# A two-layer decoder trunk on TensorE: other run lengths of high and low products, and another offset of three operand tiles

## The chip, the cores and the metric

The kernel runs on one core of one Trainium2 chip. A core has TensorE (PE in the profile; PEld is its weight load), VectorE (DVE), ScalarE (ACT), GpSimd (POOL) and SyncE (SP), which issues the transfers of the weights. The metric is the time of one execution on the device in microseconds; the time before is 2203.13 us, the median of three runs from 2200.47 to 2203.22.

## The reference

A trunk of two layers over 256 positions of width 2048, in float32. The first layer mixes by attention in a sliding window (32 query heads of 64, 8 key heads), the second by a gated linear recurrence; each ends with a gated MLP of width 6144 with a causal convolution over three positions.

```python
for layer in range(DEPTH):
    h = rmsnorm(x, mix_norm[layer])
    if layer % 2 == 0:
        x = x + sliding_window_attention(h, w_qkv, q_gain, k_gain, sinks, w_o)
    else:
        x = x + rglru_block(h, w_in, conv_w, conv_b, w_a, b_a, w_i, b_i, lam, w_out)
    h = rmsnorm(x, ffn_norm[layer])
    u = causal_dwconv(h @ w_up, conv_w, conv_b)
    g, v = split(u, 2)
    x = x + (gelu(g) * v) @ w_down
```

Nearly all the arithmetic is in the matrix products with w_qkv, w_o, w_in, w_out, w_up and w_down.

## The kernel before

Activations are held with the channels on the 128 partitions and the 256 positions (`T`) along the free axis, so a product takes a 128 x 128 block of weights as the stationary operand and streams the activations past it. To keep float32 precision at PE's faster rate, each operand is split in two float32r parts, a high one (the value cast down) and a low one (what the cast lost). An activation tile has both side by side: `h[:, k]` is 2 x 256 columns, high and low. A product of weights and activations is then two matmuls for each block k:

- a **high product** (`mm_hi`, L186 to L190): the high weights against both parts of the activations, 512 columns, into the 512 columns of one bank of the accumulator;
- a **low product** (`mm_lo`, L192 to L196): the low weights against the high part of the activations, 256 columns, added into the second half of the same bank.

Weights come in **chunks** of 128 x 2048 numbers (1 MB, 8 KB on a partition), 16 blocks each, in one fixed list `order` for the whole kernel. Each chunk goes through three steps, each with a ring of three buffers: SP issues its transfer into a `raw` tile (`dma_next`), ScalarE casts it to `hi` (`split_hi`, L115), VectorE subtracts to get `lo` (`split_lo`, L123). `advance()` does one step of each for the chunks ahead. A `hi` tile's buffer is written again for the chunk three later, after PE has read it for the last time. The order of the instructions on each engine is the order in which the program is written (`manual_schedule`); nothing is reordered by a scheduler.

The sections that the change touches, in the order of the program:

- `po`, the output projection of the attention, with `ao` as activations: chunks 2 to 15 of 16 in a plain loop, one chunk for each output block. The first two are interleaved with the end of the attention.
- `pu`, the up projection of the MLP, with `h`: two halves of 24 pairs of chunks (a gate and a value block), each pair into the two banks of one accumulator tile. In the first half the first pair is taken by `late_pair`, which leaves the last two blocks for after the norm. Each chunk is 16 high products, then 16 low ones; then comes a piece of the pair before (`step(pend)`, the epilogue `up_epi`: scale, convolution, gelu, and the split of the result into `g`), `advance()`, and another piece.
- `pd`, the down projection behind each half, with `g` as activations: eight accumulator tiles of two banks, three chunks each. A chunk has eight blocks k for each of the two banks (`i`): eight high products and eight low ones for the first bank, then eight and eight for the second. Its epilogue adds to the residual stream `x`.
- `px` and `py`, the input projections of the recurrence, with `h`, among its gates; the change leaves them as they are.
- `pr`, the output projection of the recurrence, with `z`, like `po`; then the second layer's `pu` and `pd`.

Tiles stand in SBUF in the order in which the pools are opened. In the built program `h` starts at byte 17536 of a partition (a multiple of 128), the three `hi` tiles at 86592, 94784 and 102976 and the `lo` tiles behind them (each 64 past a multiple of 128), and the pools of a section start at 135744, so that `g` is at 135744, `ao` at 160320 and `z` at 186944 (each 64 past one). The attention's smaller tiles lie behind `ao` and `z`'s place: `kq` takes 4 bytes of a 32-byte step, and the tiles `ident`, `identr`, `maskr`, `pt`, `pr`, `qsq` and `qh` behind it start on multiples of 128. All sizes along the way are multiples of 512 for the blocks of weights and of 2048 for those of activations.

Of the kernel before, what the change touches and what calls it, by code (L numbers as in the profile page):

```python
# [19 lines left out]
F32 = mybir.dt.float32  # L20
F32R = mybir.dt.float32r
AF = mybir.ActivationFunctionType
ALU = mybir.AluOpType
AX = mybir.AxisListType

P = 128
# [14 lines left out]
def trunk(ctx, tc, xT, wq, wk, wv, wo, win, wg, wout, wup, wdn, mixg, ffng, kqg, sinks,  # L41
# [9 lines left out]
    rawp = ctx.enter_context(tc.tile_pool(name="rawp", bufs=3))  # L51
    hip = ctx.enter_context(tc.tile_pool(name="hip", bufs=3))
    lop = ctx.enter_context(tc.tile_pool(name="lop", bufs=3))
    ctx.enter_context(tc.manual_schedule())

    x = per.tile([P, KD, T], F32, name="x")
# [13 lines left out]
    sp = per.tile([P, KD], F32, name="sp")  # L70
    sp4 = per.tile([P, KD], F32, name="sp4")
    sp8 = per.tile([P, KD], F32, name="sp8")


    order = []
# [117 lines left out]
    def mm_lo(ps, lo, rhs, ks, off=0, n=P, stop=True):  # L193
        for k, xk in ks:
            pe.matmul(ps[:, T:], lhsT=lo[:, off + k * n:off + k * n + P], rhs=rhs[:, xk, 0, :],  # L195
                      start=False, stop=stop and k == ks[-1][0])  # L196

    def x_epi(ps, d, n, gains, tp, out_=None, tag="xt"):

        t = tp.tile([P, n, T], F32, tag=tag, name=f"xt{st['use']}")  # L200
        xs = x[:, d:d + n, :]
        for i in ([slice(0, n)] if out_ is None else [slice(i, i + 1) for i in range(n)]):
            dve.tensor_tensor(out=t[:, i], in0=ps[:, i, 0:T], in1=xs[:, i], op=ALU.add)  # L203
            dve.tensor_tensor(out=xs[:, i], in0=ps[:, i, T:], in1=t[:, i], op=ALU.add)  # L204
            if out_ is not None:
                nc.sync.dma_start(out=out_[:, d:d + n, :][:, i], in_=xs[:, i])
        if out_ is not None:
            return
        yield
        if gains is None:  # L210
            return
        for i in range(d, d + n):
            split_x(h, x[:, i, :], gains, i)
        yield
        if n == 2:
            stat(xs, d == 0)
        elif d % 2:
            stat(x[:, d - 1:d + 1, :], d == 1)
# [35 lines left out]
    def rng(a, b):  # L254
        return [(k, k) for k in range(a, b)]
# [27 lines left out]
    with ExitStack() as ph:  # L283
# [7 lines left out]
        kz = ap_.tile([P, 4, 2, 2, T], F32R, name="kz")  # L291
        vh = ap_.tile([P, 2, 2, 512], F32R, name="vh")
        ao = ap_.tile([P, KD, 2, T], F32R, name="ao")
        kq = ap_.tile([P, 1], F32, name="kq")
        kg = ap_.tile([P, 2], F32, name="kg")
        snk = ap_.tile([P, 32], F32, name="snk")
        nsnk = ap_.tile([P, 32], F32, name="nsnk")
        cb = ap_.tile([P, T], F32, name="cb")
# [83 lines left out]
        def k_fin(p):  # L382
            s, sq = ksq.pop(p)
            pk = psT.tile([P, 512], F32, tag="pT", name=f"pk{p}")
            pe.matmul(pk[:, 0:T], lhsT=bones, rhs=sq, start=True, stop=True)
            yield
            v = a2.tile([P, T], F32, tag="ka", name=f"kv{p}")
            r = a2.tile([P, T], F32, tag="kr", bufs=1, name=f"kr{p}")
            t = a2.tile([P, T], F32, tag="kt", bufs=1, name=f"kt{p}")
            dve.scalar_tensor_tensor(out=v, in0=pk[:, 0:T], scalar=1.0 / HD, in1=cb, op0=ALU.mult, op1=ALU.add)  # L390
            rsqrt1(r, v)
            yield
            rsqrt2(r, v, t)
            dve.scalar_tensor_tensor(out=s, in0=s, scalar=kq[:, 0:1], in1=r, op0=ALU.mult, op1=ALU.mult)
            yield
            for i in range(2):
                sl = slice(64 * i, 64 * i + 64)
                act.copy(out=kz[sl, p, 0, i, :], in_=s[sl])
                dve.tensor_tensor(out=kz[sl, p, 1, i, :], in0=s[sl], in1=f(kz[sl, p, 0, i, :]), op=ALU.subtract)
# [249 lines left out]
                yield from x_epi(ps.unsqueeze(1), d, 1, gf[:, 0], a2, tag="ks")  # L649

        pend = wo_epi([(d, head[d][0]) for d in range(2)])
        for d in range(2, 16):
            hi, lo = use()
            ps = pj.tile([P, 512], F32, tag="pj", name=f"po{d}")
            mm_hi(ps, hi, ao, rng(0, KD))
            mm_lo(ps, lo, ao, rng(0, KD))
            step(pend)
            advance()
            finish(pend)
            if d == 8:  # L660
                softplus()
            pend = wo_epi([(d, ps)])
# [11 lines left out]
    def ffn(layer, nxt):  # L674
        with ExitStack() as ph:
            gp = ph.enter_context(tc.tile_pool(name=f"ffn{layer}", bufs=1, reuse_waits="tile"))
            t2 = ph.enter_context(tc.tile_pool(name=f"ffnt{layer}", bufs=2, reuse_waits="tile"))
            g = gp.tile([P, KH, 2, T], F32R, name=f"g{layer}")
            rbb = rb.unsqueeze(1).to_broadcast([P, 2, T])

            def up_epi(t, m, ps):
                a = t2.tile([P, 2, T], F32, tag="a", name=f"ua{layer}_{t}")
                s = t2.tile([P, 2, T], F32, tag="s", name=f"us{layer}_{t}")
                y = t2.tile([P, 2, T], F32, tag="y", name=f"uy{layer}_{t}")
                act.copy(out=a, in_=ps[:, :, 0:T])  # L685
                dve.tensor_tensor(out=s, in0=ps[:, :, T:], in1=a, op=ALU.add)  # L686
                dve.tensor_tensor(out=s, in0=s, in1=rbb, op=ALU.mult)  # L687
                yield
                for i in range(2):
                    n = t + i * (DFF // P)  # L690
                    act.activation(out=y[:, i, :], in_=s[:, i, :], func=AF.Identity, scale=fw[:, layer, n, 2:3],  # L691
                                   bias=fb[:, layer, n:n + 1])
                    for tap in (1, 2):
                        dve.scalar_tensor_tensor(out=y[:, i, tap:], in0=s[:, i, 0:T - tap],  # L694
                                                 scalar=fw[:, layer, n, 2 - tap:3 - tap], in1=y[:, i, tap:],
                                                 op0=ALU.mult, op1=ALU.add)
                yield
                yield
                act.activation(out=y[:, 0, :], in_=y[:, 0, :], func=AF.Gelu_apprx_tanh)
                dve.tensor_tensor(out=s[:, 0, :], in0=y[:, 0, :], in1=y[:, 1, :], op=ALU.mult)  # L700
                act.copy(out=g[:, m, 0, :], in_=s[:, 0, :])  # L701
                dve.tensor_tensor(out=g[:, m, 1, :], in0=s[:, 0, :], in1=f(g[:, m, 0, :]), op=ALU.subtract)  # L702

            pend = None
            for half in range(2):
                for m in range(KH):
                    t = half * KH + m
                    ps = mm.tile([P, 2, 512], F32, tag="mm", name=f"pu{layer}_{t}")
                    if t == 0:
                        late_pair(ps, h, lambda: norm(f"f{layer}"))  # L710
                    else:
                        for i in range(2):
                            hi, lo = use()
                            mm_hi(ps[:, i], hi, h, rng(0, KD))
                            mm_lo(ps[:, i], lo, h, rng(0, KD))
                            step(pend)
                            advance()
                            step(pend)
                    finish(pend)
                    pend = up_epi(t, m, ps)  # L720
                for dp in range(8):
                    ps = mm.tile([P, 2, 512], F32, tag="mm", name=f"pd{layer}_{half}_{dp}")
                    for c in range(3):
                        hi, lo = use()
                        ks = [(kk, 8 * c + kk) for kk in range(8)]
                        for i in range(2):
                            mm_hi(ps[:, i], hi, g, ks, off=i * P, n=2 * P, start=c == 0)
                            mm_lo(ps[:, i], lo, g, ks, off=i * P, n=2 * P, stop=c == 2)
                        step(pend)
                        advance()  # L730
                        step(pend)
                        if c == 1:
                            finish(pend)
                    pend = x_epi(ps, 2 * dp, 2, nxt if half else None, t2, None if half == 0 or nxt is not None else out)
            finish(pend)
# [3 lines left out]
    with ExitStack() as ph:  # L739
# [157 lines left out]
        for q, (what, n) in enumerate(rec_pairs):  # L897
# [10 lines left out]
                    run(after.get((q, i), ()))  # L908
            (xps if what == "x" else yps)[n] = ps

        pend = None
        for n in range(8):
            ps = mm.tile([P, 2, 512], F32, tag="mm", name=f"pr{n}")
            if n == 0:
                yproj(7)
                gated(7)
                zsplit(7)
                late_pair(ps, z)
            else:
                for i in range(2):  # L920
                    hi, lo = use()
                    mm_hi(ps[:, i], hi, z, rng(0, KD))
                    mm_lo(ps[:, i], lo, z, rng(0, KD))
                    step(pend)
                    advance()
                    step(pend)
            finish(pend)
            pend = x_epi(ps, 2 * n, 2, gf[:, 1], r2, tag="y")
# [66 lines left out]
```

## Time and profile before

| what | us |
|---|---|
| median of three runs | 2203.13 |
| the profiled execution | 2203.18 |
| its span, from the first instruction to the last | 2201.4 |
| PE busy | 2185.1 |
| VectorE busy | 1559.6 |
| ScalarE busy | 1182.0 |
| GpSimd busy | 134.0 |

The granted TensorE clock is 0.998 of full speed over the span. The weights, 401.06 MB read, come at 183 GB/s. A transfer of a chunk lands about 4.8 us after its issue. In a row of the profile `pu<-h,hi` is a matmul that writes the accumulator tile `pu` from the moving tile `h` and the stationary tile `hi`; `128x512 f32` is the size of the moving operand. The busy time of PE is not the distance from one matmul to the next: matmuls are pipelined, and a high product that is shown with 392 ns starts some 229 ns after the one before it. Distances are read from the starts in the timeline.

### The profile page before, as it was taken

How to read it: one execution, taken by the hardware profiler on the slowest of the kernel's cores; microseconds unless marked ns; L12 is line 12 of the kernel's file. 1: busy time of each engine (PE TensorE's matmuls, PEld its weight loads, DVE VectorE, ACT ScalarE, POOL GpSimd, SP SyncE). 2: the span in 40 equal slices, each digit the busy share in tenths (PEclk: the TensorE clock that was granted, in tenths of full speed). 3: DMA queues.
4: the chain of work that ended last, by engine and by line, in shares of the span. 5: the costliest groups of instructions: out<-in, count | busy, mean ns of one | idle time of the engine just before them, and what ended most of it. 6: DMA issues, size and time to landing. Idle time of an engine off the chain costs nothing.

```text
span 2201.4 us, 30745 instructions
## 1 busy us (share of the span) xinstructions
PE 2185.1 (99%) x12676; PEld 1922.7 (87%) x12676; DVE 1559.6 (71%) x1882; ACT 1182.0 (54%) x1432; POOL 134.0 (6%) x125
## 2 busy tenths in 40 slices
PE   9999999999999999999999999999999999999999
PEld 7788888888888888888888888888888888888888
DVE  6777768777644777776679877777776457777654
ACT  6677445555433555553369874455554335555432
POOL 1112220000000000002200003200000000000000
PEclk9999999999999999999999999999999999999999
DMA  7223555555555555555555546555555555555543
GB/s 272 101 96 115 192 177 206 191 191 191 191 192 188 180 192 189 191 200 183 189 211 184 186 154 213 181 194 191 191 192 191 191 177 191 191 190 191 193 187 134
DMA packets 60763, 405.14 MB, mean 184 GB/s; under 512 B 7504, under 2 KB 9936, under 8 KB 12880
## 3 DMA queue, kind: packets, MB, share of 16 engines
q1 hardware_dynamic: 60336, 403.04, 51.3%
q8 instruction: 99, 1.62, 0.3%
q14 instruction: 40, 0.33, 0.0%
q10 hardware_dynamic: 288, 0.15, 0.0%
HBM read 401.06 MB, written 2.10 MB: 183 GB/s over the span
## 4 chain that ended last, share of the span: by engine, by line
PE 98%; DVE 1%; ACT 0%; DMA 0%; issue 0%; SPq 0%; DVEq 0%
PE pu L189 32%; PE pu L195 16%; PE pd L189 16%; PE pd L195 8%; PE px L189 3%; PE py L189 3%; PE pr L189 3%; PE po L189 3%; PE pq L189 2%; PE pr L195 1%; PE po L195 1%; PE py L195 1%; PE px L195 1%; PE pq L195 1%; PE O L574 1%; PE pk L189 1%
## 5 line engine op out<-in xcount | busy, mean ns | idle before, releaser
L123 DVE TENSOR_TENSOR lo<-raw,hi 128x2048 fp32r<-128x2048 f32 (+1 forms) x390 | 856.5, 2196 | 213.7 <-ACT hi L115 206.8
L115 ACT CAST hi<-raw 128x2048 fp32r<-128x2048 f32 x373 | 712.7, 1911 | 388.4 <-PE pd L189 246.9
L189 PE MATMUL pu<-h,hi 128*128 128x512 f32 x3072 | 736.7, 392 | 0.0
L189 PEld LDWEIGHTS pu<-h,hi 128*128 128x128 f32 x3072 | 563.1, 188 | 111.2
L195 PEld LDWEIGHTS pu<-h,lo 128*128 128x128 f32 x3072 | 383.5, 188 | 16.4
L195 PE MATMUL pu<-h,lo 128*128 128x256 f32 x3072 | 387.0, 278 | 0.0
L189 PE MATMUL pd<-g,hi 128*128 128x512 f32 x1536 | 384.6, 392 | 0.0
L189 PEld LDWEIGHTS pd<-g,hi 128*128 128x128 f32 x1536 | 276.2, 189 | 49.4
L195 PEld LDWEIGHTS pd<-g,lo 128*128 128x128 f32 x1536 | 209.6, 190 | 14.9
L195 PE MATMUL pd<-g,lo 128*128 128x256 f32 x1536 | 214.2, 282 | 0.0
L701 ACT CAST g<-us 128x256 fp32r<-128x256 f32 x96 | 39.0, 406 | 280.5 <-DVE us L700 280.5
L694 DVE SCALAR_TENSOR_TENSOR uy<-us,fw,uy 128x255 f32<-128x255 f32 (+1 forms) x384 | 176.6, 480 | 6.8
L686 DVE TENSOR_TENSOR us<-pu,ua 128x512 f32<-128x512 f32 x96 | 66.4, 691 | 155.4 <-ACT ua L685 155.3
L685 ACT COPY ua<-pu 128x512 f32<-128x512 f32 x96 | 56.2, 586 | 144.3 <-PE pu L195 144.3
L691 ACT ACTIVATE uy<-us,fb,fw 128x256 f32<-128x256 f32 x192 | 105.2, 599 | 2.7 <-DVE us L687 2.7
L203 DVE TENSOR_TENSOR xt<-pd,x 128x512 f32<-128x512 f32 (+1 forms) x40 | 23.3, 582 | 82.1 <-PE pd L195 82.1
L189 PE MATMUL pq<-h,hi 128*128 128x512 f32 x256 | 73.4, 412 | 0.0
L702 DVE TENSOR_TENSOR g<-us,g 128x256 fp32r<-128x256 f32 x96 | 40.9, 426 | 45.3 <-ACT g L701 45.3
L687 DVE TENSOR_TENSOR us<-us,rb 128x512 f32<-128x512 f32 x96 | 66.4, 692 | 3.3
L160 POOL TENSOR_TENSOR sqt<-x 128x512 f32<-128x512 f32 x21 | 56.5, 2690 | 176.6 <-DVE x L204 156.9
L189 PE MATMUL po<-ao,hi 128*128 128x512 f32 x256 | 62.4, 392 | 1.1 <-DVE ao L584 1.1
L189 PE MATMUL px<-h,hi 128*128 128x512 f32 x256 | 62.3, 395 | 0.0
(214 smaller groups left out, 1838.1 us busy)
## 6 DMA issues: line engine op xcount, KB each, us to landing
raw<-in_wup SPq DMA_DIRECT2D x192, 1024.0 KB, 4.8
raw<-in_wdn SPq DMA_DIRECT2D x96, 1024.0 KB, 4.8
raw<-in_win SPq DMA_DIRECT2D x32, 1024.0 KB, 4.9
raw<-in_wq SPq DMA_DIRECT2D x16, 1024.0 KB, 4.8
raw<-in_wo SPq DMA_DIRECT2D x16, 1024.0 KB, 4.8
raw<-in_wout SPq DMA_DIRECT2D x16, 1024.0 KB, 4.7
raw<-in_wv SPq DMA_DIRECT2D x4, 1024.0 KB, 5.2
graw<-in_wg SPq DMA_DIRECT2D x8, 512.0 KB, 3.5
```

Source lines behind the costliest of these rows:

```text
L115: act.copy(out=his[c], in_=raws[c])
L123: dve.tensor_tensor(out=los[c][:, part], in0=raws[c][:, part], in1=f(his[c][:, part]), op=ALU.subtract)
L160: pool.tensor_tensor(out=sqt, in0=src, in1=src, op=ALU.mult)
L189: pe.matmul(ps, lhsT=hi[:, off + k * n:off + k * n + P], rhs=rhs[:, xk].rearrange("p a t -> p (a t)"), start=start and k == ks[0][0], stop ...
L195: pe.matmul(ps[:, T:], lhsT=lo[:, off + k * n:off + k * n + P], rhs=rhs[:, xk, 0, :], start=False, stop=stop and k == ks[-1][0])
L685: act.copy(out=a, in_=ps[:, :, 0:T])
L686: dve.tensor_tensor(out=s, in0=ps[:, :, T:], in1=a, op=ALU.add)
L687: dve.tensor_tensor(out=s, in0=s, in1=rbb, op=ALU.mult)
L691: act.activation(out=y[:, i, :], in_=s[:, i, :], func=AF.Identity, scale=fw[:, layer, n, 2:3], bias=fb[:, layer, n:n + 1])
L694: dve.scalar_tensor_tensor(out=y[:, i, tap:], in0=s[:, i, 0:T - tap], scalar=fw[:, layer, n, 2 - tap:3 - tap], in1=y[:, i, tap:], op0=ALU. ...
L701: act.copy(out=g[:, m, 0, :], in_=s[:, 0, :])
L702: dve.tensor_tensor(out=g[:, m, 1, :], in0=s[:, 0, :], in1=f(g[:, m, 0, :]), op=ALU.subtract)
```

## The change

It does three things.

- **Runs.** A new function `products` takes the place of `mm_hi` and `mm_lo` in `po`, `pu`, `pd` and `pr`. It puts a chunk's 16 high products behind those left over from the chunk before, issues the first `count` of them, then the chunk's 16 low products, and keeps the rest for the next call. `counts` gives the numbers: 14, 16, 18, then 15, 15, 18 again and again, and all that is left at the end of a section. In `pd` both banks' high products of a chunk come first and both banks' low ones behind.
- **Padding.** A pool with one tile of 64 bytes, `pad`, which nothing reads or writes, is opened behind the rings of the weights and ahead of the sections' pools. `g` then starts at byte 135808, `ao` at 160384, `z` at 187008, all multiples of 128, as `h`'s.
- **`kq`** loses its own tile: the product of the two gains is written over the first column of `kg`. The attention's tiles behind it start 32 bytes later than before, not 64: `qh` at 224800 and 226848, `pt` at 198176 and 204320, for example. `kz` and `vh`, ahead of it, move by 64.

```diff
+    gap = ctx.enter_context(tc.tile_pool(name="gap", bufs=1))
...
+    gap.tile([P, 16], F32, name="pad")
...
+    left = []
+
+    def hi_items(ps, hi, rhs, ks, off=0, n=P, start=True):
+        return [[ps, hi[:, off + k * n:off + k * n + P], rhs[:, xk].rearrange("p a t -> p (a t)"),
+                 start and k == ks[0][0], False] for k, xk in ks]
+
+    def lo_items(ps, lo, rhs, ks, off=0, n=P, stop=True):
+        return [[ps[:, T:], lo[:, off + k * n:off + k * n + P], rhs[:, xk, 0, :], False,
+                 stop and k == ks[-1][0]] for k, xk in ks]
+
+    def products(high, low, count):
+
+        run = left + high
+        count = len(run) if count is None else count
+        left[:] = run[count:]
+        if left and low[-1][4]:
+            low[-1][4], left[-1][4] = False, True
+        for ps, w, r, start, stop in run[:count] + low:
+            pe.matmul(ps, lhsT=w, rhs=r, start=start, stop=stop)
+
+    def counts(n):
+
+        c = ([14, 16, 18] + [15, 15, 18] * (n // 3))[:n]
+        c[-1] = None
+        return iter(c)
...
-        kq = ap_.tile([P, 1], F32, name="kq")
         kg = ap_.tile([P, 2], F32, name="kg")
+        kq = kg[:, 0:1]
...
+        runs = counts(14)
         for d in range(2, 16):
             hi, lo = use()
             ps = pj.tile([P, 512], F32, tag="pj", name=f"po{d}")
-            mm_hi(ps, hi, ao, rng(0, KD))
-            mm_lo(ps, lo, ao, rng(0, KD))
+            products(hi_items(ps, hi, ao, rng(0, KD)), lo_items(ps, lo, ao, rng(0, KD)), next(runs))
...
             for half in range(2):
+                runs = counts(2 * KH - 2 * (half == 0))
...
-                            mm_hi(ps[:, i], hi, h, rng(0, KD))
-                            mm_lo(ps[:, i], lo, h, rng(0, KD))
+                            products(hi_items(ps[:, i], hi, h, rng(0, KD)), lo_items(ps[:, i], lo, h, rng(0, KD)),
+                                     next(runs))
...
+                runs = counts(24)
...
+                        high, low = [], []
                         for i in range(2):
-                            mm_hi(ps[:, i], hi, g, ks, off=i * P, n=2 * P, start=c == 0)
-                            mm_lo(ps[:, i], lo, g, ks, off=i * P, n=2 * P, stop=c == 2)
+                            high += hi_items(ps[:, i], hi, g, ks, off=i * P, n=2 * P, start=c == 0)
+                            low += lo_items(ps[:, i], lo, g, ks, off=i * P, n=2 * P, stop=c == 2)
+                        products(high, low, next(runs))
```

`pr` is changed as `po` is, with `counts(14)`.

Where the instructions stand now: on PE, the start of the first half of `pu` in the first layer, behind `late_pair`. A row is the line, the operation, the tiles with their numbers (`hi42` is chunk 42's high part; `pu0_1` is pair 1 of layer 0), the size and the count. Before:

```order
L189 MATMUL pu0_1_3355<-h_70,hi42_3327 128x512 x16
L195 MATMUL pu0_1_3355<-h_70,lo42_3329 128x256 x16
L189 MATMUL pu0_1_3355<-h_70,hi43_3351 128x512 x16
L195 MATMUL pu0_1_3355<-h_70,lo43_3353 128x256 x16
L189 MATMUL pu0_2_3448<-h_70,hi44_3396 128x512 x16
L195 MATMUL pu0_2_3448<-h_70,lo44_3398 128x256 x16
```

and of the change, the same place:

```order
L221 MATMUL pu0_1_3358<-h_73,hi42_3330 128x512 x14
L221 MATMUL pu0_1_3358<-h_73,lo42_3332 128x256 x16
L221 MATMUL pu0_1_3358<-h_73,hi42_3330 128x512 x2
L221 MATMUL pu0_1_3358<-h_73,hi43_3354 128x512 x14
L221 MATMUL pu0_1_3358<-h_73,lo43_3356 128x256 x16
L221 MATMUL pu0_1_3358<-h_73,hi43_3354 128x512 x2
L221 MATMUL pu0_2_3449<-h_73,hi44_3397 128x512 x16
L221 MATMUL pu0_2_3449<-h_73,lo44_3399 128x256 x16
L221 MATMUL pu0_2_3449<-h_73,hi45_3441 128x512 x15
L221 MATMUL pu0_2_3449<-h_73,lo45_3443 128x256 x16
L221 MATMUL pu0_2_3449<-h_73,hi45_3441 128x512
```

Two high products of chunks 42 and 43 have moved behind the low products of their own chunk, to the head of the next run; the third chunk's 16 follow the two left over, a run of 18, and the first run of 15 comes next.

On PE again, the start of the down projection behind that half, with `g` as the moving tile. Before:

```order
L189 MATMUL pd0_0_0_5494<-g0_3267,hi88_5442 128x512 x8
L195 MATMUL pd0_0_0_5494<-g0_3267,lo88_5444 128x256 x8
L189 MATMUL pd0_0_0_5494<-g0_3267,hi89_5486 128x512 x8
L195 MATMUL pd0_0_0_5494<-g0_3267,lo89_5488 128x256 x8
L189 MATMUL pd0_0_0_5494<-g0_3267,hi90_5535 128x512 x8
L195 MATMUL pd0_0_0_5494<-g0_3267,lo90_5537 128x256 x8
```

(each pair of rows stands there twice, once for each bank), and of the change:

```order
L221 MATMUL pd0_0_0_5497<-g0_3270,hi88_5445 128x512 x14
L221 MATMUL pd0_0_0_5497<-g0_3270,lo88_5447 128x256 x16
L221 MATMUL pd0_0_0_5497<-g0_3270,hi88_5445 128x512 x2
L221 MATMUL pd0_0_0_5497<-g0_3270,hi89_5489 128x512 x14
L221 MATMUL pd0_0_0_5497<-g0_3270,lo89_5491 128x256 x16
L221 MATMUL pd0_0_0_5497<-g0_3270,hi89_5489 128x512 x2
L221 MATMUL pd0_0_0_5497<-g0_3270,hi90_5536 128x512 x16
L221 MATMUL pd0_0_0_5497<-g0_3270,lo90_5538 128x256 x16
```

The four short runs of a chunk have become two long ones, and the last two high products of chunks 88 and 89 stand behind the low products. On the other engines and in the DMA queue the rows stand in the same order as before; what moves there is the moment at which a cast into a released `hi` tile may start.

More of the change, by code (lines that the diff above doesn't have):

```diff
@@ L393, in k_fin @@
             rsqrt2(r, v, t)
-            dve.scalar_tensor_tensor(out=s, in0=s, scalar=kq[:, 0:1], in1=r, op0=ALU.mult, op1=ALU.mult)
+            dve.scalar_tensor_tensor(out=s, in0=s, scalar=kq, in1=r, op0=ALU.mult, op1=ALU.mult)
             yield
@@ L909, in trunk @@
             (xps if what == "x" else yps)[n] = ps
+        runs = counts(14)
         pend = None
@@ L921, in trunk @@
                     hi, lo = use()
-                    mm_hi(ps[:, i], hi, z, rng(0, KD))
-                    mm_lo(ps[:, i], lo, z, rng(0, KD))
+                    products(hi_items(ps[:, i], hi, z, rng(0, KD)), lo_items(ps[:, i], lo, z, rng(0, KD)), next(runs))
                     step(pend)
```

## The prediction

> **What bounds the kernel now.** I read the page first: busy time by engine, then the chain that ended last, then the groups. Columns of a group: line, engine, operation, out<-in, shapes, count, then busy us, mean ns of one, and idle us before it.
>
> ```profile
> span 2201.4 us, 30745 instructions
> PE 2185.1 (99%) x12676; PEld 1922.7 (87%) x12676; DVE 1559.6 (71%) x1882; ACT 1182.0 (54%) x1432; POOL 134.0 (6%) x125
> PE 98%; DVE 1%; ACT 0%; DMA 0%; issue 0%; SPq 0%; DVEq 0%
> L189 PE MATMUL pu<-h,hi 128*128 128x512 f32 x3072 | 736.7, 392 | 0.0
> L195 PE MATMUL pu<-h,lo 128*128 128x256 f32 x3072 | 387.0, 278 | 0.0
> L189 PE MATMUL pd<-g,hi 128*128 128x512 f32 x1536 | 384.6, 392 | 0.0
> L195 PE MATMUL pd<-g,lo 128*128 128x256 f32 x1536 | 214.2, 282 | 0.0
> ```
>
> PE is the bound: 98% of the chain is its own, and the products of up and down projections have no idle time before them. Nothing outside PE can shorten the kernel; only the distance from one matmul's start to the next can. The change leaves the matmuls, their sizes and their number as they were, so the question is whether that distance depends on the order of the products or on the addresses. The timeline of PE, merged by tile, gives it (start, length with the last one's tail, name, count; I use only differences of starts).
>
> ```profile
> 724.66 3.84 PE L189 MATMUL pu<-h,hi 128*128 128x512 f32 x16
> 728.33 1.98 PE L195 MATMUL pu<-h,lo 128*128 128x256 f32 x16
> 730.15 3.82 PE L189 MATMUL pu<-h,hi 128*128 128x512 f32 x16
> 733.81 2.05 PE L195 MATMUL pu<-h,lo 128*128 128x256 f32 x16
> 735.69 3.84 PE L189 MATMUL pu<-h,hi 128*128 128x512 f32 x16
> 739.37 1.98 PE L195 MATMUL pu<-h,lo 128*128 128x256 f32 x16
> 741.18 3.82 PE L189 MATMUL pu<-h,hi 128*128 128x512 f32 x16
> ```
>
> Chunks of the up projection alternate. The sixteen low products last 1.82 us (728.33 to 730.15), then 1.88 (733.81 to 735.69), then 1.81, with the same tiles, shapes and buffers in rotation. Two chunks take 735.69 - 724.66 = 11.03 us. What differs is where the high run before them stopped. The next rows are single queries of windows so narrow that one matmul alone was running, and of the low runs behind; the last number but one is the duration. First the last high product before the low run at 904.87 and that run, then the first three products of the next high run, its sixteenth, and the low run behind it.
>
> ```profile
> L189 PE MATMUL pu<-h,hi 128*128 128x512 f32 x1 | 0.4, 394 | 0.0
> L195 PE MATMUL pu<-h,lo 128*128 128x256 f32 x14 | 1.7, 276 | 0.0
> ...
> L189 PE MATMUL pu<-h,hi 128*128 128x512 f32 x1 | 0.4, 388 | 0.0
> L189 PE MATMUL pu<-h,hi 128*128 128x512 f32 x1 | 0.4, 392 | 0.0
> L189 PE MATMUL pu<-h,hi 128*128 128x512 f32 x1 | 0.4, 394 | 0.0
> ...
> L189 PE MATMUL pu<-h,hi 128*128 128x512 f32 x1 | 0.4, 388 | 0.0
> L195 PE MATMUL pu<-h,lo 128*128 128x256 f32 x14 | 1.8, 280 | 0.0
> ```
>
> High products come in three kinds, 388, 392, 394 ns, in turn. A run that stops on the 394 kind is followed by quick low products (276); the next high run then begins with 388 again. Sixteen is 5 x 3 + 1, so that run ends on 388, and slow low products follow (280). A run of 15 or 18 that begins on 388 ends on 394: all its low products would be quick, and the next run begins on 388 again.
>
> **Part 1, the runs of 15, 15, 18.** Three chunks have 48 high products and 3 x 16 low ones, as before. In the quick state a high run of 16 takes 3.66 us (730.15 to 733.81), so 48 take 10.98; a quick low run takes 1.815 (the mean of 1.82 and 1.81). Per chunk that is 10.98/3 + 1.815 = 5.475 us, against 11.03/2 = 5.515 now. Saved: 0.040 us on each of the 188 up chunks that go through the new code (46 + 48 in each of two layers), **7.5 us**.
>
> **Part 2, the padding.** Now h starts on a multiple of 128 bytes, the weights' tiles 64 bytes past one, and g, ao and z also 64 past; after the padding g, ao and z stand like h. The down projection reads g, the last projection of the second mixer reads z:
>
> ```profile
> 696.76 2.00 PE L189 MATMUL pd<-g,hi 128*128 128x512 f32 x8
> 698.60 1.11 PE L195 MATMUL pd<-g,lo 128*128 128x256 f32 x8
> 699.55 2.00 PE L189 MATMUL pd<-g,hi 128*128 128x512 f32 x8
> 701.39 1.11 PE L195 MATMUL pd<-g,lo 128*128 128x256 f32 x8
> 702.34 2.00 PE L189 MATMUL pd<-g,hi 128*128 128x512 f32 x8
> ...
> 1342.14 3.82 PE L189 MATMUL pr<-z,hi 128*128 128x512 f32 x16
> 1345.80 2.08 PE L195 MATMUL pr<-z,lo 128*128 128x256 f32 x16
> 1347.71 3.82 PE L189 MATMUL pr<-z,hi 128*128 128x512 f32 x16
> ```
>
> A chunk with z takes 1347.71 - 1342.14 = 5.57 us and its low run 1.91, longer than either kind with h, in runs of the very same length. A chunk with g, in runs of 8, takes 702.34 - 696.76 = 5.58. If the offset is the cause, both fall to 5.475: 96 down chunks x 0.105 = **10.1 us**, and 14 chunks with z and 14 with ao (which I take to be like z's) x 0.095 = **2.7 us**. Runs of 16 with g would not do that by themselves: z has them, and 5.57.
>
> **Part 3, what it costs.** Each of the ten sections with the new runs (ao, four up, four down, z) has to fall into step, by 14, 16, 18. From "begins on 388", 14 ends on the second kind and not the third, so I charge three slow chunks a section at 5.54 (730.15 to 735.69): 10 x 3 x 0.065 = **2.0 us** lost.
>
> The up to two products left over move behind the low run, so a high tile is released about two microseconds later, and ScalarE's cast of the chunk three behind it, which writes into the same buffer, starts later; everything behind that cast in ScalarE's queue, and VectorE's low part after it, moves along. The tightest place is the start of a down section, where the last slice of g stands in ScalarE's queue behind such a cast (start, length, what; idle before, releaser):
>
> ```profile
> 578.68 1.91 ACT L115 CAST hi<-raw 128x2048 fp32r<-128x2048 f32 x1 [1.25 <-PE pd L189]
> 580.50 0.41 ACT L699 ACTIVATE uy<-uy 128x256 f32<-128x256 f32 x1
> 583.73 0.42 DVE L702 TENSOR_TENSOR g<-us,g 128x256 fp32r<-128x256 f32 x1 [0.47 <-ACT g L701]
> 579.44 2.00 PE L189 MATMUL pd<-g,hi 128*128 128x512 f32 x8
> 585.02 2.00 PE L189 MATMUL pd<-g,hi 128*128 128x512 f32 x8
> ```
>
> The cast waited for PE until 578.68, and the last slice of g was done at 584.15; PE reads it first in the eighth product of the run at 585.02, 7 x 0.229 later, at 586.62: 2.5 us to spare. After the change the cast waits for two products at the head of the run that now starts at 579.44, about 579.44 + 0.46 + 0.2 = 580.1, 1.4 us later, while PE reads that slice two products later and its chunks end 0.2 us earlier: 2.5 - 1.4 + 0.46 - 0.2 = 1.3 us remain. I cost it at nothing; with the cover gone it would be a microsecond or so at each of four such places. Elsewhere the cast serves a chunk two later, 11 us off, with more room. The DMA queue on SP and GpSimd see the same order of work; a raw tile comes free as much later as the low part ends.
>
> Taking out the 4-byte tile moves everything behind it in the attention pools by 32 bytes against 64-byte steps, in all by 32 and not 64. No matmul of the trace reads a tile that starts 32 bytes past a multiple of 64. These do afterwards:
>
> ```profile
> L574 PE MATMUL O<-pt,vh 128*128 128x256 f32 x144 | 19.7, 281 | 0.0
> L556 PE MATMUL pT<-ident,pr 128*128 128x128 f32 x96 | 16.2, 281 | 0.0
> L502 PE MATMUL S<-maskr,identr 128*128 128x512 f32 (+1 forms) x32 | 12.3, 384 | 0.0
> L505 PE MATMUL S<-kz,qh 128*128 128x512 f32 (+1 forms) x32 | 11.3, 354 | 0.0
> ```
>
> With the two other lines of the scores (L503 and L504, 32 each) that is 144 + 96 + 4 x 32 = 368 matmuls. The nearest measured effect of an offset is z's low product against h's quick one, (1.91 - 1.815)/16 = 6 ns: -2.2 to +2.2 us. Relative offsets change both ways here, so I take nothing and keep both ends.
>
> **The sum.** -7.5 - 10.1 - 2.7 + 2.0 = -18.3 us, from this execution's own 2203.18 (span 2201.4 and 1.8 around it; the median of the runs, 2203.13, is the same): **2184.9 us**.
>
> **A rule that speaks against it.** The trace has 1.815, 1.88 and 1.91 us for sixteen low products of one shape. The Trainium skill, SBUF — State Buffer, section Who interferes with whom, gives PE two independent read ports, one for the moving operand and one for the weights, and says that PE never waits on anyone; by it an offset between the two is worth nothing, and part 2 falls away. The trace bears more against that rule than for it, since z and h differ in nothing else that I see. As a mechanism of this kernel it is the second rival.
>
> **Rivals.**
> 1. The offset works but the step in threes isn't kept, say because a run now crosses from one accumulator bank to the next. Up chunks stay at 5.515; the others fall to that: 96 x 0.065 + 28 x 0.055 = 7.8 saved, 2195.4 us. Against it: low to high already crosses banks at each chunk, and the kinds run on.
> 2. The offset is not the cause and something else of g and z is. Then part 1 alone holds, with 96 x 0.01 for g's runs of 16: 8.5 - 1.0 for five or so up and down starts, 2195.7 us.
> 3. The change does nothing: the kinds fall out of step at once and the offset is not the cause. 2200 to 2205 us.
> 4. Slower: the 32-byte offset makes each of the 368 attention matmuls read its tiles in more pieces. It undoes the gain from 18.3/368 = 50 ns each; if it doubled them, from some 0.11 us, the price would be 40 us: 2225. Nothing in the trace reads such an offset, so nothing excludes it; the effect of the one offset that is seen is 6 ns.
>
> **How the numbers follow.** Forecast 72%, 2180.5 to 2190 (attention at either end, no or double the cost of starts); rivals 1 and 2 7% each; rival 3 7%; rival 4 7%. Range 2180.5 to 2197, which takes in the first three. Faster by over 0.2% (4.4 us, about what a measurement of this kernel can tell from no change): 0.72 + 0.14 = 0.86; within it 0.07; slower 0.07.
>
> **What would show it.** In the timeline of after: up chunks with runs of 15, 15, 18 and low runs all at 1.81 us, 16.43 us for three chunks; the same for pd, po and pr; low products of pd at a mean of 276 ns, not 282. Slow low runs (1.88) only in the first three or four chunks of a section. No idle time before the first pd products that read the last slice of g. It would be wrong if low runs after 15 or 18 came out at 1.88 (rival 1), if pd and pr kept 1.91 (rival 2), or if O, S and pT grew (rival 4).

## The result, and the profile after

The change takes 2181.06 us (median of four runs, 2179.87 to 2182.43) against 2201.87 for four runs of before: a ratio of 0.9903, with a 95% interval from 0.9890 to 0.9917. The forecast was 2184.9, the range 2180.5 to 2197.0.

The page of the change, the rows that answer to those of before (busy us, mean ns of one, idle before):

```profile
span 2179.7 us, 30745 instructions
PE 2163.9 (99%) x12676; PEld 1904.1 (87%) x12676; DVE 1565.2 (72%) x1882; ACT 1175.0 (54%) x1432; POOL 133.7 (6%) x125
L221 PE MATMUL pu<-h,lo 128*128 128x256 f32 x3008 | 372.3, 276 | 0.0
L221 PE MATMUL pd<-g,hi 128*128 128x512 f32 x1536 | 367.3, 391 | 0.0
L221 PE MATMUL pd<-g,lo 128*128 128x256 f32 x1536 | 190.3, 276 | 0.0
```

PE is as full as before, with the same 12676 matmuls, and 21.7 us of span are gone. The low products of pd have a mean of 276 ns in place of 282, those of pu 276 in place of 278. The timeline of PE shows three chunks of pu, then one of pd and one of pr:

```profile
344.95 4.28 PE L221 MATMUL pu<-h,hi 128*128 128x512 f32 x18
349.07 1.98 PE L221 MATMUL pu<-h,lo 128*128 128x256 f32 x16
350.88 3.60 PE L221 MATMUL pu<-h,hi 128*128 128x512 f32 x15
354.32 1.98 PE L221 MATMUL pu<-h,lo 128*128 128x256 f32 x16
356.13 3.60 PE L221 MATMUL pu<-h,hi 128*128 128x512 f32 x15
359.56 1.98 PE L221 MATMUL pu<-h,lo 128*128 128x256 f32 x16
361.38 0.85 PE L221 MATMUL pu<-h,hi 128*128 128x512 f32 x3
...
608.17 3.60 PE L221 MATMUL pd<-g,hi 128*128 128x512 f32 x15
611.61 1.98 PE L221 MATMUL pd<-g,lo 128*128 128x256 f32 x16
613.42 4.28 PE L221 MATMUL pd<-g,hi 128*128 128x512 f32 x18
...
1329.68 3.60 PE L221 MATMUL pr<-z,hi 128*128 128x512 f32 x15
1333.12 1.98 PE L221 MATMUL pr<-z,lo 128*128 128x256 f32 x16
1334.93 4.28 PE L221 MATMUL pr<-z,hi 128*128 128x512 f32 x18
```

Every low run shown takes 1.81 or 1.82 us, with h, g and z alike; in these sections the alternation is gone but for their starts and ends. Three chunks of pu take 361.38 - 344.95 = 16.43 us, 5.477 each. A chunk of pd with 15 high products takes 613.42 - 608.17 = 5.25, one of pr 1334.93 - 1329.68 = 5.25: the same to the last digit.

Where the time went, section by section, from the first product of a section to the first of the next in PE's timeline (us; the four parts of pu and of pd added up; the last part of pd reaches to the end of the span). The other columns are the experiments below.

| section | before | change | e1 pad | e2 runs | e3 14, 17 | e4 12, 18 | e5 ahead | e6 gates | e7 32 B | e8 threes |
|---|---|---|---|---|---|---|---|---|---|---|
| start and attention | 212.42 | 211.21 | 210.89 | 210.09 | 210.72 | 209.80 | 210.89 | 210.19 | 212.47 | 211.00 |
| po | 95.64 | 94.74 | 94.99 | 95.68 | 95.49 | 94.49 | 95.79 | 94.65 | 96.30 | 94.49 |
| pu | 1061.50 | 1054.20 | 1061.22 | 1054.54 | 1068.48 | 1053.72 | 1070.52 | 1054.20 | 1054.12 | 1053.39 |
| pd | 541.01 | 531.02 | 534.19 | 539.08 | 538.24 | 530.52 | 539.08 | 531.02 | 542.35 | 530.36 |
| recurrence | 201.78 | 200.52 | 201.01 | 201.78 | 201.10 | 200.52 | 202.03 | 201.68 | 200.44 | 200.92 |
| pr | 89.07 | 88.00 | 88.26 | 89.07 | 88.75 | 88.01 | 89.07 | 88.00 | 89.70 | 88.06 |
| span | 2201.4 | 2179.7 | 2190.6 | 2190.2 | 2202.8 | 2177.0 | 2207.4 | 2179.7 | 2195.4 | 2178.2 |

Of the 21.7 us, pd gives 10.0, pu 7.3, pr 1.1 and po 0.9: 19.3 in the sections that the change rewrites. The recurrence gives 1.3 though its code is untouched, and the start and attention 1.2, which come and go by up to 2.7 us among all these runs, with the padding and without. The granted clock was 0.997 to 0.999 in the profiled executions of all ten programs, so it explains none of the differences between them.

### The profile page after: what moved, and what is told of

Read it like the earlier page. It is cut to its first block, busy times and chain, and to the rows that moved or that the text cites. A ratio compares the mean times of both kernels' runs of the same rounds, so it can differ in the third digit from the quotient of the medians.

```text
span 2179.7 us, 30745 instructions
## 1 busy us (share of the span) xinstructions
PE 2163.9 (99%) x12676; PEld 1904.1 (87%) x12676; DVE 1565.2 (72%) x1882; ACT 1175.0 (54%) x1432; POOL 133.7 (6%) x125
## 4 chain that ended last, share of the span: by engine, by line
PE 98%; DVE 1%; ACT 0%; DMA 0%; issue 0%; SPq 0%; DVEq 0%
PE pu L221 47%; PE pd L221 24%; PE po L221 4%; PE pr L221 4%; PE py L192 3%; PE px L192 3%; PE pq L192 2%; PE px L198 1%; PE py L198 1%; PE pq L198 1%; PE pk L192 1%; PE O L605 1%; PE pu L192 1%; PE pT L587 0%; PE pk L198 0%; PE g L841 0%
## 5 line engine op out<-in xcount | busy, mean ns | idle before, releaser
L221 PE MATMUL pu<-h,hi 128*128 128x512 f32 x3008 | 719.1, 391 | 0.0
L221 PEld LDWEIGHTS pu<-h,hi 128*128 128x128 f32 x3008 | 551.0, 188 | 107.6
L221 PEld LDWEIGHTS pu<-h,lo 128*128 128x128 f32 x3008 | 369.6, 188 | 16.1
L221 PE MATMUL pu<-h,lo 128*128 128x256 f32 x3008 | 372.3, 276 | 0.0
L221 PE MATMUL pd<-g,hi 128*128 128x512 f32 x1536 | 367.3, 391 | 0.0
L221 PEld LDWEIGHTS pd<-g,hi 128*128 128x128 f32 x1536 | 281.4, 188 | 55.0
L221 PEld LDWEIGHTS pd<-g,lo 128*128 128x128 f32 x1536 | 188.9, 188 | 8.2
L221 PE MATMUL pd<-g,lo 128*128 128x256 f32 x1536 | 190.3, 276 | 0.0
L161 POOL TENSOR_TENSOR sqa<-x 128x512 f32<-128x512 f32 x3 | 6.9, 2300 | 901.1 <-DVE x L235 901.1
L192 PE MATMUL py<-h,hi 128*128 128x512 f32 x256 | 61.3, 392 | 0.0
```

What stands on the lines that cost most here:

```text
L192: pe.matmul(ps, lhsT=hi[:, off + k * n:off + k * n + P], rhs=rhs[:, xk].rearrange("p a t -> p (a t)"), start=start and k == ks[0][0], stop ...
L221: pe.matmul(ps, lhsT=w, rhs=r, start=start, stop=stop)
```

## The experiments

The theory: the length of the high runs modulo three and the distance between the places of the moving tile and of the weights modulo 128 bytes set the time from one matmul to the next; together they give the gain. Rivals: only one of the two parts works; long runs across chunk borders are what helps, not their length modulo three; it is the place of the moving tile and not its distance from the weights.

**e1: the padding alone.** Runs of 16 (8 in pd) as before.

```diff
+    gap = ctx.enter_context(tc.tile_pool(name="gap", bufs=1))
...
+    gap.tile([P, 16], F32, name="pad")
...
-        kq = ap_.tile([P, 1], F32, name="kq")
         kg = ap_.tile([P, 2], F32, name="kg")
+        kq = kg[:, 0:1]
```

> The padding and the shared kq tile alone, with runs of 16 (8 in pd) as before. If the distance between moving tile and weights modulo 128 bytes decides: po and pr fall from 5.57 us a chunk to pu's alternation of 5.49 and 5.54 (mean 5.515), pd with its runs of 8 to one slow and one quick low run a chunk, about 5.51, and the input projections of the recurrence gain the same 1.3 us as with the change; pu stays at 5.515. In all 96 x 0.07 + 28 x 0.055 + 1.3 = 9.5 us below before. If the offset is worth nothing and the runs do everything: pd and pr stay at 5.58 and 5.57, the time is that of before.

Measured: 2192.39 us against 2202.01 for before in the same series, ratio 0.9958 (0.9944 to 0.9973). PE's timeline of pd in e1:

```profile
596.48 1.99 PE L192 MATMUL pd<-g,hi 128*128 128x512 f32 x8
598.31 1.11 PE L198 MATMUL pd<-g,lo 128*128 128x256 f32 x8
599.25 2.00 PE L192 MATMUL pd<-g,hi 128*128 128x512 f32 x8
601.09 1.07 PE L198 MATMUL pd<-g,lo 128*128 128x256 f32 x8
601.99 1.99 PE L192 MATMUL pd<-g,hi 128*128 128x512 f32 x8
```

A chunk takes 601.99 - 596.48 = 5.51 us with one slow low run (0.94) and one quick (0.90), as expected. pu stays within 0.3 us of before. The offset works by itself: the median is 9.6 us lower, and in the table 9.0 of that stand in pd (6.8), pr (0.8), po (0.6) and the recurrence (0.8). The recurrence was expected to gain 1.3; e6 below comes back to that.

**e2: the runs alone.** From the change:

```diff
-    gap = ctx.enter_context(tc.tile_pool(name="gap", bufs=1))
...
-    gap.tile([P, 16], F32, name="pad")
...
+        kq = ap_.tile([P, 1], F32, name="kq")
         kg = ap_.tile([P, 2], F32, name="kg")
-        kq = kg[:, 0:1]
```

> The runs of 15, 15, 18 alone; g, ao and z start 64 bytes past a multiple of 128 as the weights do. If both parts are needed for g: pu falls to 5.475 us a chunk (7.5 us less in all), pd only to 5.566 (low products of 120 ns whatever the high run's length; 1.8 us less), px and py stay as before; about 9 us below before. If the runs alone bring pd's gain: pd at 5.475 and the time within 2 us of the change's.

Measured: 2192.57 us, ratio 0.9959 (0.9944 to 0.9974). The same place in pd:

```profile
586.69 3.59 PE L219 MATMUL pd<-g,hi 128*128 128x512 f32 x15
590.12 2.08 PE L219 MATMUL pd<-g,lo 128*128 128x256 f32 x16
...
597.37 4.27 PE L219 MATMUL pd<-g,hi 128*128 128x512 f32 x18
601.48 2.08 PE L219 MATMUL pd<-g,lo 128*128 128x256 f32 x16
603.39 0.86 PE L219 MATMUL pd<-g,hi 128*128 128x512 f32 x3
```

The high runs are 15 and 18 long and the low runs still take 1.91 us: (603.39 - 586.69)/3 = 5.567 us a chunk. The runs are worth 7.0 us in pu and 1.9 in pd; po, pr and the recurrence are those of before. In pd the padding alone saves 6.8 us (e1) and the runs alone 1.9; both together save 10.0, more than the 8.7 of the two apart.

**e3: as many products across the borders, lengths that are no multiple of three.**

```diff
-        c = ([14, 16, 18] + [15, 15, 18] * (n // 3))[:n]
+        c = ([14, 17, 17] * (n // 3 + 1))[:n]
```

> The change with runs of 14, 17, 17 in place of 14, 16, 18 and 15, 15, 18: as many products cross chunk borders, none of the lengths is a multiple of three. If the step in threes decides: every run ends on the wrong kind, all low runs take 1.88 us, three chunks 16.67 us in place of 16.43, so about 24 us above the change, 2205, no better than before. If long runs over chunk borders, or fewer changes between high and low, are the gain: within 2 us of the change.

Measured: 2205.20 us, ratio 1.0014 (1.0005 to 1.0023), 24 us above the change. Three chunks of pu in e3:

```profile
356.47 4.06 PE L221 MATMUL pu<-h,hi 128*128 128x512 f32 x17
360.37 2.05 PE L221 MATMUL pu<-h,lo 128*128 128x256 f32 x16
362.25 4.06 PE L221 MATMUL pu<-h,hi 128*128 128x512 f32 x17
366.15 2.05 PE L221 MATMUL pu<-h,lo 128*128 128x256 f32 x16
368.04 3.38 PE L221 MATMUL pu<-h,hi 128*128 128x512 f32 x14
371.25 2.05 PE L221 MATMUL pu<-h,lo 128*128 128x256 f32 x16
373.14 1.09 PE L221 MATMUL pu<-h,hi 128*128 128x512 f32 x4
```

All low runs take 1.88 or 1.89 us and three chunks 373.14 - 356.47 = 16.67, as expected. Crossing chunk borders is worth nothing by itself; with the wrong lengths the whole gain is given back, padding and all.

**e4: other multiples of three.**

```diff
-        c = ([14, 16, 18] + [15, 15, 18] * (n // 3))[:n]
+        c = ([12, 18, 18] * (n // 3 + 1))[:n]
```

> The change with runs of 12, 18, 18 throughout: multiples of three, with up to four products left over. If the step in threes decides: three chunks take 16.43 us as with the change, and sections that begin in step are in step from their first run (up to three slow low runs fewer in each): 0 to 1.5 us below the change. If a later release of the high tiles costs something, this shows more of it: idle time at the start of pd, above the change.

Measured: 2179.29 us, ratio 0.9900 (0.9883 to 0.9916). Four products left over in place of two cost nothing, and the second parts of pu and pd, which begin in step, are 0.25 us shorter each; from 226 us on PE waits only once, 1.1 us in po, as in the change. In the sections that the change rewrites the table gives 1.2 us less than with the change. The start and the attention take 1.4 less, but they vary by more than that among the runs. The two intervals overlap, so the times alone don't tell e4 from the change.

**e5: the padding ahead of the weights.** g, ao and z stay where the change puts them, and the weights' rings move by 64 bytes.

```diff
+    gap = ctx.enter_context(tc.tile_pool(name="gap", bufs=1))
+    gap.tile([P, 16], F32, name="pad")
     rawp = ctx.enter_context(tc.tile_pool(name="rawp", bufs=3))
...
-    gap = ctx.enter_context(tc.tile_pool(name="gap", bufs=1))
```

> The change with its 64 bytes ahead of the weights' rings in place of behind them: the weights' tiles now start on multiples of 128, as h, g, ao and z do. If the distance between moving tile and weights decides, and not the place of either: h's products fall to what g's were with the runs alone, low products at 120 ns, 5.566 us a chunk in pu and pd alike; 312 x 0.09 and one or two more in px, py and pq, about 2210, slower than before. If it were the moving tile's own place on a multiple of 128: as with the change, 2181.

Measured: 2210.18 us against 2201.88, ratio 1.0038 (1.0023 to 1.0053). pu in e5:

```profile
352.07 3.59 PE L221 MATMUL pu<-h,hi 128*128 128x512 f32 x15
355.50 2.08 PE L221 MATMUL pu<-h,lo 128*128 128x256 f32 x16
357.41 3.59 PE L221 MATMUL pu<-h,hi 128*128 128x512 f32 x15
...
368.77 0.40 PE L221 MATMUL pu<-h,hi 128*128 128x512 f32 x1
```

Three chunks take 368.77 - 352.07 = 16.70 us, 5.567 each, and the low run 357.41 - 355.50 = 1.91, now with h, whose own address has not changed. So the moving tile's own place does not decide; the distance to the weights fits. The products of the recurrence's gates fit too: their weights and their moving tile xc always move together, 64 past a multiple of 128 in e6 and on one in the change, and they follow each other every 0.12 us in both (1123.61 to 1123.73 and 1124.72 to 1124.84). The one pairing that was not run is weights on a multiple of 128 with the moving tile 64 past one.

**e6: the gates' tiles back at their old offset.** The padding is opened inside each section; in the recurrence it comes behind the tiles of the gates, of which PE reads ghi, glo and xc.

```diff
-    gap = ctx.enter_context(tc.tile_pool(name="gap", bufs=1))
...
-    gap.tile([P, 16], F32, name="pad")
...
+        gap = ph.enter_context(tc.tile_pool(name="gapz", bufs=1))
+        gap.tile([P, 16], F32, name="padz")
         zp = ph.enter_context(tc.tile_pool(name="z", bufs=1, reuse_waits="tile"))
```

> The change with the padding opened inside each section, in the recurrence behind the gates' tiles and ahead of z: only the gates' tiles (ghi, glo, xc) are back at 64 past a multiple of 128. If the 1.3 us that px and py gained come from the state in which the gates' products leave PE: the recurrence takes 201.8 us again in place of 200.5, each high run behind gates begins with products of 233 ns, and all else is as with the change (2182). If they come from late_pair ahead of them: 200.5.

Measured: 2181.33 us; the recurrence takes 201.68 us, against 200.52 with the change and 201.78 before. The first product run behind a group of gates in e6, then in the change:

```profile
1126.49 3.90 PE L190 MATMUL px<-h,hi 128*128 128x512 f32 x16
1130.22 2.05 PE L196 MATMUL px<-h,lo 128*128 128x256 f32 x16
```

```profile
1127.60 3.82 PE L192 MATMUL px<-h,hi 128*128 128x512 f32 x16
1131.26 2.05 PE L198 MATMUL px<-h,lo 128*128 128x256 f32 x16
```

3.73 us for sixteen high products (1126.49 to 1130.22) in place of 3.66: 233 ns each. It is the same behind all eight groups of gates. So 1.2 of the 1.3 us that the recurrence gained hang on the gates' own tiles, which the padding also moved. They are two halves. The eight high runs behind gates take 3.66 us in place of 3.74, 0.6 us in all, in e1 too. And of the 30 low runs of px and py that have 16 products, 16 are slow with the change, 24 before and in e6, but 23 in e1: this second half comes with the runs of the change and not with those of before (e1) or of e3, where 23 are slow too. So e1 gained 0.8.

**e7: 32 bytes in place of 64.**

```diff
-    gap.tile([P, 16], F32, name="pad")
+    gap.tile([P, 8], F32, name="pad")
```

> The change with 32 bytes of padding: g, ao and z start 32 bytes past the weights modulo 128, and the attention's tiles stand where they stood before. If what counts is the half of 128 bytes in which a tile starts: pd at 5.566 us a chunk as with the runs alone, about 2191. If any distance will do: pd at 5.476, 2181.

Measured: 2196.66 us, ratio 0.9975 (0.9965 to 0.9986). Neither expectation holds. pd in e7:

```profile
589.72 3.66 PE L221 MATMUL pd<-g,hi 128*128 128x512 f32 x15
593.22 2.05 PE L221 MATMUL pd<-g,lo 128*128 128x256 f32 x16
...
606.53 0.86 PE L221 MATMUL pd<-g,hi 128*128 128x512 f32 x3
```

(606.53 - 589.72)/3 = 5.603 us a chunk, worse than with no padding at all (5.567): fifteen high products take 3.50 us, 233 ns each, in place of 3.43 or 3.44. For g a distance of 32 is a third case and the worst one seen; why stays open. The whole is still faster than before, above all since pu keeps the gain of its runs.

**e8: threes everywhere.** The runs also in px and py, and a start of 14 behind `late_pair` alone.

```diff
-        c = ([14, 16, 18] + [15, 15, 18] * (n // 3))[:n]
+        c = (([14] + [18, 15, 15] * n) if late else ([12, 18, 18] * n))[:n]
...
-                    mm_hi(ps[:, i], hi, h, rng(0, KD))
-                    mm_lo(ps[:, i], lo, h, rng(0, KD))
+                    products(hi_items(ps[:, i], hi, h, rng(0, KD)), lo_items(ps[:, i], lo, h, rng(0, KD)), next(runs))
                     run(before.get((q, i), ()))
```

> The change with runs of 12, 18, 18 where a section begins in step, of 14 and then 18, 15, 15 behind late_pair, and the same in px and py. If the step in threes is all of it: px and py lose their alternation (16 of 32 slow low runs, 0.065 us each, 1.0 us), the sections their slow starts (another 1 us or so against the change): about 2179, the recurrence 199.5 us. If the gates between the runs put PE out of step: the recurrence stays at 200.5.

Measured: 2180.49 us, ratio 0.9905 (0.9889 to 0.9922), not to be told from the change. The recurrence takes 200.92 us, neither 199.5 nor 200.5. VectorE and PE in e8 at the place of PE's only wait in that section, then the same place in the change, and last a cast on ScalarE some 50 us earlier in e8:

```profile
1174.51 2.29 DVE L126 TENSOR_TENSOR lo<-raw,hi 128x2048 fp32r<-128x2048 f32 x1
1175.79 0.28 PE L839 MATMUL g<-xc,ghi 128*128 128x256 f32 x1
1176.71 0.68 DVE L813 TENSOR_TENSOR xc<-y,xc 128x512 fp32r<-128x512 f32 x1
1177.45 0.39 PE L840 MATMUL g<-xc,ghi 128*128 128x256 f32 x1 [1.37 <-DVE xc L813]
```

```profile
1176.72 0.68 DVE L813 TENSOR_TENSOR xc<-y,xc 128x512 fp32r<-128x512 f32 x1
1177.49 0.28 PE L839 MATMUL g<-xc,ghi 128*128 128x256 f32 x1
```

```profile
1126.42 1.91 ACT L118 CAST hi<-raw 128x2048 fp32r<-128x2048 f32 x1 [2.65 <-PE px L221]
```

The products are in step (fifteen slow low runs fewer), which saves 1.0 us, and a single wait of 1.4 us takes it back. The gates need the low part of xc, which stands behind a chunk's low part on VectorE. VectorE does that at the same moment in both (1176.71 and 1176.72), but PE comes to the gates 1.7 us sooner in e8 (1175.79 and 1177.49). VectorE had entered the section 1.2 us ahead of the change as well, and lost it where a high product that was put off came to stand behind a group of gates: the cast into its tile waited 2.65 us, where the change's cast, at 1124.90, waited for nothing, and VectorE waited for ScalarE in turn. VectorE is busy for 172.9 of the 200.5 us of this section with the change, and had not won that back by then.

## Why the prediction was right, point by point

Both mechanisms are the ones that were forecast. The time, 2181.06 us, is 3.8 us below the forecast of 2184.9 and 0.6 above the lower end of the range. The forecast started from the profiled 2203.18; the four runs of before that stand beside the change have a median of 2201.87. From profile to profile the span fell by 21.7 us, 3.4 more than the 18.3 of the sum (rounded parts): 1.0 in the sections that the change rewrites, 1.3 in the recurrence, and 1.2 in the start and the attention, which no run ties to the change.

- **The step in threes** (7.5 us, less 0.8 for the four starts): measured 7.3 in pu. e3 and e4 show that it is the length modulo three. Rival 1 (a run over two banks falls out of step) is refuted by the 16.43 us, rival 3 (no effect) by the time.
- **The offset** (10.1 in pd, 2.7 in po and pr, less their starts): measured 10.0 and 2.0. e1 shows that the offset is a cause, e5 that the moving tile's own place is not it, so rival 2 falls. But the term held more than the offset, since it let these chunks drop straight to 5.475: of the 12.0 us the padding alone gives 8.3 (e1) and the runs alone 1.9 (e2). The rule of the Trainium skill (SBUF — State Buffer, Who interferes with whom) is that PE never waits on anyone. By that rule the distance should be worth nothing. Here sixteen low products of one shape take 1.81 or 1.91 us by it, and the measurement decides; how the place of one operand comes to matter to the other no run shows.
- **The starts** (2.0 us): nearly right, by another count. e8, whose sections begin in step, takes 1.7 us less than the change in po, pu, pd and pr. The change has 27 slow low runs there and not 30. Five sections begin in step and have three each, as foreseen. The three behind `late_pair` have two, and pd behind the first half of pu has one, in each layer. The last run of four sections, of 16 or 17 products, is followed by a slow one too, which the sum did not charge. This is pd behind the first half:

```profile
569.98 3.38 PE L221 MATMUL pd<-g,hi 128*128 128x512 f32 x14
573.19 2.04 PE L221 MATMUL pd<-g,lo 128*128 128x256 f32 x16
575.08 3.84 PE L221 MATMUL pd<-g,hi 128*128 128x512 f32 x16
578.75 1.98 PE L221 MATMUL pd<-g,lo 128*128 128x256 f32 x16
580.57 2.68 PE L221 MATMUL pd<-g,hi 128*128 128x512 f32 x11
```

  The run behind the 14 ends in step (580.57 - 578.75 = 1.82). I had charged all sections as if they began on 388; this one follows a last run of 16 that ended out of step, from which 14, 16, 18 falls in sooner. So the starts give 0.3 of the 1.0 us; the rest is the gain per chunk, read at one place to two decimals: in e8 pd is 10.7 us below before (10.1 charged), pu 8.1 (7.5), po and pr 2.2 (2.7).
- **The cast that starts later**, at the same place, ScalarE and VectorE in the change:

```profile
575.74 1.92 ACT L118 CAST hi<-raw 128x2048 fp32r<-128x2048 f32 x1 [2.19 <-PE pd L221]
580.79 0.43 DVE L733 TENSOR_TENSOR g<-us,g 128x256 fp32r<-128x256 f32 x1 [0.47 <-ACT g L732]
```

  The last slice of g is done at 581.22. PE reads it in the tenth product of the run at 580.57, at 580.57 + 9 x 0.229 = 582.63: 1.4 us to spare, 1.3 were foreseen, and PE waits for nothing there. That the two figures agree so well is luck. Counted from the start of the section, the cast starts 0.9 us later than before and not 1.4, and the slice is read 0.1 earlier and not 0.3 later: I forgot that a run which puts off two products also ends 0.46 us sooner, and the slip stood on both sides. e8 shows what such a delay costs where there is no room.
- **The 32-byte offset in the attention** (nothing, -2.2 to +2.2): right. O has a mean of 281 ns before and 281 after, pT 281 and 283, and attention without the start takes 179.8 and 179.7 us. Rival 4 is refuted.
- **Missed**: 1.3 us in the recurrence. I followed the padding to g, ao and z and not to the gates' tiles, behind which the next high run is 0.07 us quicker (e6). The 1.1 us by which the values' first product came earlier (32.65 to 31.52 us) lies in the loading before it and varies among these runs between 30.9 and 32.7 us without regard to the change.

Still open: why the kinds come in threes, what the distance of 32 bytes does, and whether 128 bytes is the period. By the addresses given above, every distance between a moving tile and a block of weights in these sections is 0, 32 or 64 bytes modulo 512 as well.

## What to carry to other kernels

Where PE is full and its idle time is nil, look at the distance between starts, by run: equal shapes with unequal distances are time to be had. Try the distance of the moving tile from the weights in small steps, and count where a run stops before a change of size. Every matmul that is put off keeps a buffer, so follow the queue behind the engine that refills it.

## What the runs showed of the hardware

Distances between matmuls of one shape depended on where both operands lie: sixteen low products of 256 columns took 1.81 us in step and 1.88 out of step with 64 bytes between the tiles' places modulo 128, and 1.91 with none, behind 15, 16 and 18 high products alike. With 32, high products took 233 ns each in place of 229. The pattern outlasts a change of accumulator bank and of chunk, and other products in between set it anew: with the gates' tiles at the weights' own offset modulo 128, the next sixteen high products took 3.73 us, with the tiles 64 bytes further on 3.66.
